# End of layer 0 in a two-layer attention step: gated y chunks loaded two steps ahead, output projection by groups of pairs

## The chip, the cores and the metric

One core of a Trainium2 chip runs the whole program in one launch. The metric is device time in microseconds, lower is better. The kernel before has a median of 2044.95 us over 3 runs (2044.95 to 2046.53).

## The reference, cut to what matters

```
for i in range(2):                       # layer 0: differential attention, layer 1: latent attention
    sh, sc, gt = split(silu(cond) @ w_ada[i] + b_ada[i])     # "ada": 3 x 1024 modulation columns
    h = rmsnorm(x, g_pre[i]) * (1 + sc) + sh
    o = attention_i(h @ w_in)            # 8 heads, 1024 latent and 256 prompt tokens
    y = rmsnorm(o, g_sub) * silu(gate)   # layer 0: per head
    x = x + gt * rmsnorm(y @ w_out[i], g_post[i])
```

Everything is float32. There are 1280 tokens, 1024 columns, 8 heads. Outputs are x after both layers and the keys and values of the prompt.

## The kernel before, in words

Tokens go in five pairs of 128-token tiles: pairs 0 to 3 are latent, pair 4 (`CTXP`) is the prompt. A float32 product is made of three matmuls on a high and a low part (`mm3`, L319 to L321), so each weight tile is loaded into a staging tile `wst` (3 buffers), cast to `wh` on ScalarE (L311), and its rest `wl` is computed on GpSimd or VectorE (L312); `wh` and `wl` have 5 buffers each and one item of work uses 4.

The heads of layer 0 run one after the other. A head has nine units: two for each latent pair and one for the prompt. A unit has scores (L590, L598), row maxima on VectorE (L592, L599), exponentials (L604), the combination of the two softmaxes on VectorE (L635), transposes (L658), their split (L660, L661) and, for each pair, the product with v. In between, a `Feeder` mixes in other matmuls: a list of items, `P2`, each with a planned cost, and every unit gets a share of the planned total in proportion to the weights `FEV`, `FOD`, `FX`. The items are columns of v (`v1`), of the gate (`g0`), modulation chunks (`a0` to `a7`, each 8 matmuls of 32 rows, L185, a copy of their sum on VectorE, L205, and four small matmuls, L230) and last `y3`: the last quarter of the gate, with the y chunks. A modulation matmul is planned at `AC` = 480 ns, three matmuls of a gate column at 360 ns.

A y chunk (`y_chunk`) is 256 columns of a pair: y and the gate are loaded from DRAM (L739), multiplied on GpSimd (L740), transposed on TensorE (L749), and split by ScalarE and VectorE (L750, L751). Fifteen chunks are placed in `y3`, by a table `at` of step counts; five more (the columns of the last two heads) follow, two of them (for pairs 3 and 4) in the output projection, on tiles called `xt`.

The output projection of layer 0 (`out_items`) has four items of 256 columns; each goes over all five pairs, with the weights of the next item requested while the last pair runs. At the last item a pair is complete: x is loaded, the residual is added (`residual`, L952 to L967), x1 is stored (L1514), its norm is taken in place (`norm_pair`, L255 to L262) and a generator of four steps of transposes (`norm_pair_to_hT`, L282 to L291) goes into a queue, `Later`: it may begin `HD` = 28 steps after that, one step in every three, where a step is three matmuls. The first projection of layer 1 (`ev_kva`) then takes the pairs in order and first finishes what the queue still holds for its pair.

The order of instructions on each engine is fixed when the program is built; engines wait for each other by semaphores.

Of the kernel before, what the change touches and what calls it, by code (L numbers as in the profile page):

```python
# [17 lines left out]
P = 128  # L18
D = 1024
# [62 lines left out]
class K:  # L82
    P1 = "k0 q0 k1 q1 k2 q2 k3 q3"
    P2 = "v1 a0 a1 v2 g0 a2 v3 a3 g1 a4 a6 g2 a5 a7 y3"
# [645 lines left out]
    def y_chunk(self, pr, kk, late=None):  # L730
# [12 lines left out]
        if pr not in self.yT:  # L743
# [11 lines left out]
    def gate_y_item(self, hp):  # L755
# [7 lines left out]
        def gen(ws):  # L763
            gs = [self.y_chunk(pr, kk) for pr in range(NPAIR) for kk in range(3)]
            at = [34 + 4 * n for n in range(6)] + [64 + 2 * n for n in range(6)] + [99] * 5

            def step(n):
                if n < len(gs):
                    next(gs[n])
                return next(gs[n - 1]) if 1 <= n < len(gs) + 1 else 0  # L770
            n = cnt = 0
            for v in gate(ws):
                if v is not None:
                    cnt += 1
                    if cnt >= at[n]:
                        v += step(n)
                        n += 1
                yield v
            for n in range(n, len(gs) + 1):
# [3 lines left out]
    def l0_items(self):  # L783
# [5 lines left out]
        def item(x):  # L789
# [5 lines left out]
            if k == "y":  # L795
                return self.gate_y_item(j), 80 * 360 + 15 * 440
# [3 lines left out]
    def l0_heads(self, items):  # L800
# [88 lines left out]
    def gp_rows(self, pool, l, cond, ps, pstag):  # L889

        nc = self.nc
        gp = self.t(pool, [P, D], f"gp{cond if l else 0}")
        for half in range(2):
# [4 lines left out]
            nc.scalar.copy(gp[:, half * 512:(half + 1) * 512], pt.rearrange("p a b -> p (a b)"))  # L898
        return gp
# [759 lines left out]
```

## Time and profile before

| what | value |
|---|---|
| median of 3 runs | 2044.95 us |
| the profiled execution | 2044.24 us, of it a span of 2042.4 us |
| TensorE busy | 1926.0 us (94%) |
| VectorE busy | 1241.2 us (61%) |
| ScalarE busy | 957.9 us (47%) |
| GpSimd busy | 513.1 us (25%) |

TensorE is busy for nearly all of the span, and the chain that ended last runs almost only over it. So the numbers that matter are the gaps on TensorE, and the stretches in which its granted clock is 0.50 of full speed. Times below count from the start of the span. The heads of layer 0 end at about 998 us, the output projection of layer 0 runs to about 1138 us, and the first projection of layer 1 follows it.

### The profile page before, as it was taken

To read this page: it belongs to the slowest core of one execution; us is meant where nothing else is said; L and a number is where in the kernel's file an instruction comes from. 1 tells how busy PE (TensorE), PEld (TensorE's weight loads), DVE (VectorE), ACT (ScalarE), POOL (GpSimd) and SP (SyncE) were. 2 spreads that over 40 slices of the span, in tenths; PEclk is the share of its full clock that TensorE was granted. 3 is DMA by queue.
4 is the path that set the end of the run, shared out by engine and by line. 5 is a ranking of instruction groups with operands and counts; after the bars stand their busy time and mean duration, and the time that the engine had idled before them with its cause. 6 is when DMAs were issued, how large, how long until landed. Compare 5 with 4: busy or idle time off the path is not lost. (4 is left out here: it accounts for less than half of the span.)

```text
span 2042.4 us, 36029 instructions
## 1 busy us (share of the span) xinstructions
PE 1926.0 (94%) x13472; PEld 1732.5 (85%) x13472; DVE 1241.2 (61%) x2503; ACT 957.9 (47%) x2401; POOL 513.1 (25%) x733
## 2 busy tenths in 40 slices
PE   6899999999999999998698899999999999999998
PEld 4788888798988978887698798888999889998998
DVE  4543447788778777788314823247776876777413
ACT  4422124666666666666324633234544444556421
POOL 3354442222122122224313532011000110003214
PEclk8999999999999999999899999999999999999999
DMA  8555544455355353544413212210101001012412
GB/s 305 157 165 187 175 150 145 146 148 146 116 155 184 103 173 113 172 131 140 141 43 115 94 55 68 73 55 21 36 24 32 22 23 41 27 37 91 149 64 104
DMA packets 207086, 220.85 MB, mean 108 GB/s; under 512 B 23776, under 2 KB 171584, under 8 KB 206784
## 3 DMA queue, kind: packets, MB, share of 16 engines
q1 hardware_dynamic: 206608, 218.51, 34.1%
q8 instruction: 106, 1.74, 0.4%
q14 instruction: 68, 0.56, 0.1%
q10 hardware_dynamic: 304, 0.05, 0.0%
HBM read 148.95 MB, written 69.53 MB: 107 GB/s over the span
## 5 line engine op out<-in xcount | busy, mean ns | idle before, releaser
L319 PE MATMUL pj<-wh,hh 128*128 128x256 f32 (+1 forms) x1264 | 368.8, 292 | 5.8 <-DVE hh L290 2.8
L320 PE MATMUL pj<-wl,hh 128*128 128x256 f32 (+1 forms) x1264 | 359.1, 284 | 4.1 <-POOL wl L312 1.8
L321 PE MATMUL pj<-wh,hl 128*128 128x256 f32 (+1 forms) x1264 | 359.7, 285 | 2.0 <-POOL hl L291 1.9
L319 PEld LDWEIGHTS pj<-wh,hh 128*128 128x128 f32 x1264 | 242.1, 192 | 10.9 <-DVE hh L290 4.3
L320 PEld LDWEIGHTS pj<-wl,hh 128*128 128x128 f32 x1264 | 242.5, 192 | 5.5 <-POOL wl L312 3.3
L321 PEld LDWEIGHTS pj<-wh,hl 128*128 128x128 f32 x1264 | 242.0, 191 | 5.0 <-POOL hl L291 3.6
L312 POOL TENSOR_TENSOR wl<-wst,wh 128x512 fp32r<-128x512 f32 (+3 forms) x90 | 104.2, 1166 | 560.2 <-ACT wh L311 456.1
L592 DVE TENSOR_REDUCE mA<-S 128x1 f32<-128x1024 f32 x128 | 155.6, 1219 | 58.4 <-PE S L590 57.7
L321 PE MATMUL pj<-hh,wl 128*128 128x512 f32 (+1 forms) x512 | 188.5, 368 | 0.4 <-POOL wl L352 0.3
L319 PE MATMUL pj<-hh,wh 128*128 128x512 f32 (+1 forms) x512 | 188.3, 368 | 0.0
L320 PE MATMUL pj<-hl,wh 128*128 128x512 f32 (+1 forms) x512 | 187.8, 367 | 0.0
L604 ACT ACTIVATE e<-S,bias 128x1024 f32<-128x1024 f32 x128 | 142.8, 1116 | 93.4 <-DVE bias L601 91.0
L590 PE MATMUL S<-kl,q 128*128 128x512 f32 x512 | 152.9, 419 | 4.6 <-ACT e L604 3.0
L660 ACT CAST pth<-tp 128x512 fp32r<-128x512 f32 (+1 forms) x208 | 99.6, 512 | 84.3 <-PE tp L658 83.4
L660 ACT CAST pth<-pj 128x512 fp32r<-128x512 f32 (+1 forms) x192 | 98.2, 518 | 79.6 <-PE pj L658 78.0
L635 DVE SCALAR_TENSOR_TENSOR e<-e,cf,e 128x512 f32<-128x512 f32 (+1 forms) x192 | 127.1, 700 | 1.1
L661 DVE TENSOR_TENSOR ptl<-tp,pth 128x512 fp32r<-128x512 f32 (+1 forms) x208 | 116.0, 581 | 14.1 <-ACT pth L660 13.4
L243 POOL TENSOR_SCALAR orsv<-oss 128x2 f32<-128x2 f32 x40 | 8.1, 202 | 433.2 <-ACT oT L688 433.1
L661 DVE TENSOR_TENSOR ptl<-pj,pth 128x512 fp32r<-128x512 f32 (+1 forms) x192 | 112.9, 592 | 5.5 <-ACT pth L660 5.2
L658 PE MATMUL pj<-identr,e 128*128 128x128 f32 x640 | 109.1, 279 | 6.9 <-DVE ptl L661 4.0
L321 PEld LDWEIGHTS pj<-hh,wl 128*128 128x128 f32 x512 | 96.3, 188 | 20.3 <-POOL wl L352 3.2
L590 PEld LDWEIGHTS S<-kl,q 128*128 128x128 f32 x512 | 90.8, 196 | 23.4 <-ACT e L604 6.1
(325 smaller groups left out, 5342.1 us busy)
## 6 DMA issues: line engine op xcount, KB each, us to landing
q<-qsd SPq DMA_DIRECT2D x320, 64.0 KB, 2.0
wst<-in_da_w_in_dram SPq DMA_DIRECT2D x64, 256.0 KB, 3.1
kl<-ksd SPq DMA_DIRECT2D x64, 192.0 KB, 3.9
ast<-in_w_ada_dram SPq DMA_DIRECT2D x8, 1024.0 KB, 9.2
wh<-in_w_ada_dram SPq DMA_DIRECT2D x32, 256.0 KB, 2.8
wl<-in_w_ada_dram SPq DMA_DIRECT2D x32, 256.0 KB, 3.1
wst<-in_w_out_dram SPq DMA_DIRECT2D x32, 256.0 KB, 2.6
vdh<-s SPq DMA_DIRECT2D x24, 256.0 KB, 2.1
```

Source lines behind the costliest of these rows:

```text
L243: nc.gpsimd.tensor_scalar(out=v, in0=ss, scalar1=1.0 / n, scalar2=EPS, op0=ALU.mult, op1=ALU.add)
L312: (lo_engs or [nc.gpsimd])[k0 // kb % len(lo_engs or [0])].tensor_tensor(out=wl, in0=st, in1=f32(wh), op=ALU.subtract)
L319: nc.tensor.matmul(out, a[0], b[0], start=first, stop=False)
L320: nc.tensor.matmul(out, a[0], b[1], start=False, stop=False)
L321: nc.tensor.matmul(out, a[1], b[0], start=False, stop=last)
L590: nc.tensor.matmul(S[:, so:so + 512], st(cc, o), kl[cc][:, so:so + 512], start=(o == 0), stop=(o == 1))
L592: nc.vector.reduce_max(out=mA[:, cc:cc + 1], in_=S, axis=AX.X)
L604: nc.scalar.activation(u.es[cc][:, 0:1024], A[cc], AF.Exp, bias=bias[:, cc:cc + 1], scale=0.125, accum_out=u.zA[:, cc:cc + 1])
L635: nc.vector.scalar_tensor_tensor(out=w[:, sl], in0=w[:, sl], scalar=cf, in1=e0[:, sl], op0=ALU.mult, op1=ALU.add)
L658: nc.tensor.transpose(tp[:, j, :], u.e[:, (c0 + j) * P:(c0 + j + 1) * P], self.ident)
L660: nc.scalar.copy(hi, tp[:, 0:cn, :])
L661: nc.vector.tensor_tensor(out=u.ptl[g][:, 0:cn, u.i * P:(u.i + 1) * P], in0=tp[:, 0:cn, :], in1=f32(hi), op=ALU.subtract)
```

## The change

```diff
-    P2 = "v1 a0 a1 v2 g0 a2 v3 a3 g1 a4 a6 g2 a5 a7 y3"
+    P2 = "v1 a0 a1 v2 g0 a2 v3 a3 g1 a4 a5 g2 y3"
+    YA = (6, 7)
+    YS = [32 + 4 * n for n in range(6)] + [60 + 2 * n for n in range(6)] + [78 + 3 * n for n in range(5)]
-    HD, HE = 28, 3
+    HD, HE, ND = 44, 3, 12
-    AC = 480.0
+    AC = 215.0
+    OUT0, OUT1 = ((0, 1, CTXP), (2, 3)), (tuple(range(NPAIR)),)
+    ORD1 = OUT0[0] + OUT0[1]
@@ y_chunk: every second chunk on two of the weights' staging tiles; three steps
+        elif alt:
+            y, g = (self.t(self.wp, [P, 2, 256], "wst", bufs=3) for j in range(2))
         for o, src in ((y, self.ydram), (g, self.gdram)):
             nc.sync.dma_start(...)
+        yield 1
         nc.gpsimd.tensor_tensor(out=y, in0=y, in1=g, op=ALU.mult)
         yield 1
+        if late:
+            yield 1
@@ gate_y_item
-            at = [34 + 4 * n for n in range(6)] + [64 + 2 * n for n in range(6)] + [99] * 5
             def step(n):
-                if n < len(gs):
-                    next(gs[n])
-                return next(gs[n - 1]) if 1 <= n < len(gs) + 1 else 0
+                for j in range(3):
+                    if 0 <= n - j < len(gs):
+                        next(gs[n - j], None)
+                return 440 if n >= 2 else 0
-            for v in gate(ws):
+            for v in self.chain([(lambda: ws, gate)] + more):
@@ l0_heads
-        post, yc, ylist = iter(()), None, list(range(NPAIR))
+        post, yc, ylist = iter(()), None, [0, 1, 2, CTXP, 3]
+            if yc:
+                next(yc)
@@ out_items, l1_tok_item: the pairs of a group, in its order
-                for pr in range(NPAIR):
+                for pr in prs:
-        return [item(n) for n in range(4)]
+        return [item(n, prs) for prs in groups for n in range(4)]
@@ run
+        def load_x(pr):
...
+            x0s[pr] = x0, xt
+        def norm(pr):
             self.norm_pair(xs[pr], yp, sp)
+            yield
+        later, norms, x0s = Later(self.HE), Later(1), {}
+        for prs in self.OUT0:
+            prefetch[2, prs[-1]] = prs[0]
+            prefetch.update({(3, a): b for a, b in zip(prs, prs[1:])})
             if n == 3:
...
                 x_pair(pr, zz, gp)
+                norms.add(norm(pr), self.ND, pr)
+                later.add(turn(pr), self.HD, ("h", pr))
+            if (n, pr) in prefetch:
+                load_x(prefetch[n, pr])
```

The columns of the gate `gp` also become two pieces (768 and 256 wide), and the prompt's are put into tiles of x. The number of matmuls stays the same. Since there are two groups of pairs, the output weights of layer 0 are loaded and split twice: 16 loads of 256 KB more, 16 casts on ScalarE, 8 subtractions on VectorE and 8 on GpSimd.

Three places show how the order moves. In these rows the changed kernel has its own line numbers: L189 is L185 of before, L234 is L230, L594 is L590, L662 is L658, L759 is L749, L908 is L896, L316 is L312, L266 is L262, L978 is L959, L986 is L967.

TensorE, the end of the first modulation chunk, before (`silc` is the conditioning, `sel` adds up the four row groups, `S` are scores):

```order
L185 MATMUL pj_3924<-wh_3652,silc_231 32x512
L658 MATMUL pj_3932<-identr_219,e_3711 128x128 x4
L598 MATMUL pj_3940<-kl_3052,q_3774 128x256 x2
L598 MATMUL pj_3940<-kl_3053,q_3774 128x256 x2
L658 MATMUL pj_3954<-identr_219,e_3711 128x128 x2
L185 MATMUL pj_3924<-wl_3653,silc_231 32x512
L185 MATMUL pj_3924<-wh_3654,silc_231 32x512
L185 MATMUL pj_3924<-wl_3655,silc_231 32x512
L230 MATMUL pj_4004<-sel_234,s_4002 128x2 x4
L185 MATMUL pj_4011<-wh_3983,silc_231 32x512
```

and with the change:

```order
L189 MATMUL pj_3977<-wl_3709,silc_231 32x512
L189 MATMUL pj_3977<-wh_3710,silc_231 32x512
L189 MATMUL pj_3977<-wl_3711,silc_231 32x512
L594 MATMUL S_4030<-kl_3052,q_3765 128x512 x4
L234 MATMUL pj_4004<-sel_234,s_4002 128x2 x4
L189 MATMUL pj_4011<-wh_3983,silc_231 32x512
```

Four score matmuls now stand between the last modulation matmul and the small ones that wait for VectorE's copy of the sum. Over all eight chunks, before, three had nothing in between and the other five 18 to 54 matmuls; with the change one has nothing (the fourth), the others 4, 8, 17, 32, 32, 48 and 60.

TensorE, the end of head 7, before (`kl` are y chunks, `e` the last unit's weights, `pth` and `vh` its product with v):

```order
L896 MATMUL xt_12135<-identr_219,ada_127_236 128x128 x2
L749 MATMUL pj_11960<-identr_219,kl_11923 128x128 x4
L749 MATMUL pj_11967<-identr_219,kl_11850 128x128 x4
L896 MATMUL xt_12135<-identr_219,ada_127_236 128x128
L896 MATMUL xt_12141<-identr_219,ada_127_236 128x128 x4
L749 MATMUL pj_11984<-identr_219,kl_11956 128x128 x4
L658 MATMUL pj_11991<-identr_219,e_11780 128x128 x4
L658 MATMUL pj_11998<-identr_219,e_11780 128x128 x4
L658 MATMUL pj_12005<-identr_219,e_11780 128x128 x2
L749 MATMUL pj_12014<-identr_219,kl_11978 128x128 x4
L749 MATMUL pj_12021<-identr_219,kl_12010 128x128 x4
L319 MATMUL pj_12028<-pth_2521_11854,vh_10961 128x256
```

and with the change:

```order
L189 MATMUL pj_11987<-wl_11924,silc_231 32x512
L189 MATMUL pj_11987<-wh_11925,silc_231 32x512
L189 MATMUL pj_11987<-wl_11926,silc_231 32x512
L189 MATMUL pj_11987<-wh_11927,silc_231 32x512
L759 MATMUL pj_11992<-identr_219,kl_11877 128x128 x4
L189 MATMUL pj_11987<-wl_11928,silc_231 32x512
L662 MATMUL pj_12005<-identr_219,e_11807 128x128 x4
L189 MATMUL pj_11987<-wh_11929,silc_231 32x512
L662 MATMUL pj_12013<-identr_219,e_11807 128x128 x4
L189 MATMUL pj_11987<-wl_11930,silc_231 32x512
L662 MATMUL pj_12020<-identr_219,e_11807 128x128 x2
L323 MATMUL pj_12028<-pth_2523_11881,vh_10963 128x256
```

The two chunks straight ahead of the last product with v are gone from there, and the last modulation chunk (L189) stands between the transposes.

VectorE, where pairs 0 and 1 are complete, before (`xt` and `z` are the two pieces of x, L952 to L967 the residual, L262 the norm; the first two x tiles are pair 0's):

```order
L952 SCALAR_TENSOR_TENSOR rsv_13169<-zss_2592_12180 128x2
L959 SCALAR_TENSOR_TENSOR ztmp_13173<-pj_13110,rs_13171,gp_2569_12134 128x256
L967 SCALAR_TENSOR_TENSOR z_2591_12179<-z_2591_12179,rs_13171,x_2691_13163 128x768
L959 SCALAR_TENSOR_TENSOR ztmp_13177<-pj_13110,rs_13171,gp_2569_12134 128x256
L967 SCALAR_TENSOR_TENSOR z_2591_12179<-z_2591_12179,rs_13171,x_2692_13164 128x768
L262 TENSOR_SCALAR xt_13165<-xt_13165,rs_13195 128x256 x2
L952 SCALAR_TENSOR_TENSOR rsv_13260<-zss_2597_12236 128x2
L959 SCALAR_TENSOR_TENSOR ztmp_13264<-pj_13201,rs_13262,gp_2569_12134 128x256
L967 SCALAR_TENSOR_TENSOR z_2596_12235<-z_2596_12235,rs_13262,x_2708_13254 128x768
L959 SCALAR_TENSOR_TENSOR ztmp_13268<-pj_13201,rs_13262,gp_2569_12134 128x256
L262 TENSOR_SCALAR z_2591_12179<-z_2591_12179,rs_13195 128x768 x2
L967 SCALAR_TENSOR_TENSOR z_2596_12235<-z_2596_12235,rs_13262,x_2709_13255 128x768
```

and with the change:

```order
L986 SCALAR_TENSOR_TENSOR z_2598_12187<-z_2598_12187,rs_12845,x_2673_12784 128x768
L978 SCALAR_TENSOR_TENSOR ztmp_12851<-pj_12790,rs_12845,gp_2576_12141 128x256
L986 SCALAR_TENSOR_TENSOR z_2598_12187<-z_2598_12187,rs_12845,x_2674_12785 128x768
L266 TENSOR_SCALAR xt_12786<-xt_12786,rs_12912 128x256 x2
L971 SCALAR_TENSOR_TENSOR rsv_12934<-zss_2606_12248 128x2
L978 SCALAR_TENSOR_TENSOR ztmp_12938<-pj_12863,rs_12936,gp_2576_12141 128x256
L986 SCALAR_TENSOR_TENSOR z_2605_12247<-z_2605_12247,rs_12936,x_2683_12857 128x768
L978 SCALAR_TENSOR_TENSOR ztmp_12942<-pj_12863,rs_12936,gp_2576_12141 128x256
L266 TENSOR_SCALAR z_2598_12187<-z_2598_12187,rs_12912 128x768 x2
L986 SCALAR_TENSOR_TENSOR z_2605_12247<-z_2605_12247,rs_12936,x_2684_12858 128x768
L316 TENSOR_TENSOR wl_12961<-wst_12962,wh_12960 128x512
L316 TENSOR_TENSOR wl_12973<-wst_12974,wh_12972 128x512
```

Behind the norm of pair 0 and the residual of pair 1 there now come the two low parts of the weights with which the second group begins. On TensorE the first transposes of pair 0 come 132 matmuls after its last projection matmul, where they were 87 behind it.

## Rows read from the trace of the kernel before

**Rows 1.** Busy time by engine in stretches, granted TensorE clock, DMA share.

```profile
core 0: us, PE busy (x) PEld busy (x) DVE busy (x) ACT busy (x) POOL busy (x), PEclk, DMA share, GB/s
410.00:560.00 150.00, 147.64 (x1112) 138.15 (x1112) 123.06 (x251) 100.71 (x268) 30.27 (x60) 1.00 0.47 139
...
850.00:900.00 50.00, 43.52 (x287) 33.63 (x286) 40.72 (x78) 31.28 (x81) 16.32 (x25) 1.00 0.49 153
900.00:968.00 68.00, 60.98 (x458) 55.96 (x456) 54.74 (x101) 43.49 (x109) 23.17 (x34) 1.00 0.47 139
968.00:998.00 30.00, 17.34 (x108) 15.32 (x107) 16.15 (x25) 13.15 (x33) 14.20 (x15) 0.77 0.44 142
...
1015.00:1095.00 80.00, 80.00 (x688) 80.00 (x687) 13.88 (x18) 22.89 (x72) 11.09 (x22) 1.00 0.15 46
1095.00:1176.00 81.00, 65.68 (x502) 62.42 (x502) 59.13 (x126) 49.56 (x129) 43.35 (x58) 0.94 0.37 121
```

**Rows 2.** The same view of the stretches with a granted clock of 0.50.

```profile
389.80:396.60 6.80, 6.80 (x19) 4.44 (x20) 4.72 (x9) 3.52 (x9) 1.27 (x1) 0.50 0.92 297
662.90:669.70 6.80, 6.22 (x22) 5.54 (x23) 4.39 (x8) 4.28 (x10) 0.37 (x1) 0.50 0.82 194
...
778.90:782.30 3.40, 3.40 (x19) 3.40 (x18) 1.80 (x6) 1.56 (x5) 0.01 (x1) 0.50 0.41 115
980.30:994.00 13.70, 8.24 (x39) 7.44 (x38) 4.51 (x7) 3.51 (x6) 6.27 (x5) 0.50 0.66 211
1011.00:1014.40 3.40, 3.02 (x14) 3.02 (x15) 0.75 (x1) 0.69 (x1) 0.61 (x2) 0.51 0.56 175
1110.00:1113.40 3.40, 3.40 (x18) 3.40 (x17) 1.40 (x4) 2.77 (x8) 1.55 (x4) 0.50 0.87 287
1151.00:1157.80 6.80, 6.05 (x29) 6.06 (x30) 4.89 (x14) 5.53 (x18) 4.34 (x9) 0.50 0.36 102
```

**Rows 3.** TensorE's waits, 300 to 850 us: total us, times, longest.

```profile
PE pj L230 <- DVE s L205: 8.6, 3, 3.6
```

**Rows 4.** TensorE in order of time, 850 to 900 us: start, us, idle before.

```profile
867.65 1.20 PE L590 MATMUL S<-kl,q 128*128 128x512 f32 x4 [0.76 <-ACT e L604]
```

**Rows 5.** TensorE's waits, 850 to 968 us.

```profile
PE pj L749 <- POOL kl L740: 3.9, 2, 2.4
```

**Rows 6.** TensorE's waits, 900 to 1015 us.

```profile
PE pj L749 <- POOL kl L740: 11.9, 5, 4.1
PE pj L749 <- POOL xt L740: 4.4, 1, 4.4
...
PE pj L319 <- DVE hl L751: 1.4, 1, 1.4
```

**Rows 7.** GpSimd in order of time, 966 to 1013 us.

```profile
1010.06 1.26 POOL L740 TENSOR_TENSOR xt<-xt,xt 128x512 f32<-128x512 f32 x1 [9.16 <-DMA xt<-g]
```

**Rows 8.** TensorE's waits, 1095 to 1176 us.

```profile
PE xt L282 <- ACT hfull L289: 9.5, 7, 4.5
PE xt L282 <- DVE z L262: 3.9, 2, 3.3
PE pj L320 <- DVE wl L312: 1.6, 1, 1.6
```

**Rows 9.** VectorE in order of time, 1090 to 1180 us.

```profile
1096.29 0.16 DVE L952 SCALAR_TENSOR_TENSOR rsv<-zss 128x2 f32<-128x2 f32 x1 [5.61 <-ACT junk L926]
...
1107.85 1.61 DVE L262 TENSOR_SCALAR z<-z,rs 128x768 f32<-128x768 f32 x2
1109.38 1.01 DVE L967 SCALAR_TENSOR_TENSOR z<-z,rs,x 128x768 f32<-128x768 f32 x1
```

**Rows 10.** Weight splits (L312) of 1015 to 1176 us: ns min/median/max.

```profile
L312 DVE TENSOR_TENSOR wl<-wst,wh x8: 679/912/1754, 1032.1 to 1135.1; 128x512 fp32r<-128x512 f32 x8
```

**Rows 11.** VectorE by shape, softmax combination, 300 to 960 us: count, busy us, mean ns.

```profile
L635 DVE SCALAR_TENSOR_TENSOR e<-e,cf,e 128x512 f32<-128x512 f32 x124 | 94.7, 787 | 1.0
```

**Rows 12.** The same group in 966 to 973 us, beside two GpSimd multiplications (L740).

```profile
L635 DVE SCALAR_TENSOR_TENSOR e<-e,cf,e 128x512 f32<-128x512 f32 x3 | 4.2, 1412 | 0.1
```

More of the change, by code (lines that the diff above doesn't have):

```diff
@@ L728, in pt_tiles, with y_chunk @@
             u.pth, u.ptl = prev.pth, prev.ptl
-    def y_chunk(self, pr, kk, late=None):
+    def y_chunk(self, pr, kk, late=None, alt=False):
         nc, c = self.nc, self.c
@@ L753, in y_chunk, with gate_y_item @@
         yield 440
-    def gate_y_item(self, hp):
+    def gate_y_item(self, hp, more):
         self.gated = -1
@@ L763, in gen @@
         def gen(ws):
-            gs = [self.y_chunk(pr, kk) for pr in range(NPAIR) for kk in range(3)]
-            at = [34 + 4 * n for n in range(6)] + [64 + 2 * n for n in range(6)] + [99] * 5
+            gs = [self.y_chunk(pr, kk, alt=(3 * pr + kk) % 2) for pr in range(NPAIR) for kk in range(3)]
+            at = self.YS
             def step(n):
-                if n < len(gs):
-                    next(gs[n])
-                return next(gs[n - 1]) if 1 <= n < len(gs) + 1 else 0
+                for j in range(3):
+                    if 0 <= n - j < len(gs):
+                        next(gs[n - j], None)
+                return 440 if n >= 2 else 0
             n = cnt = 0
-            for v in gate(ws):
[L773 to L777, printed above, removed]
+            for v in self.chain([(lambda: ws, gate)] + more):
+                cnt += 1
+                while n < len(at) and cnt >= at[n]:
+                    v += step(n)
+                    n += 1
                 yield v
-            for n in range(n, len(gs) + 1):
+            for n in range(n, len(gs) + 2):
                 yield step(n)
@@ L795, in item @@
             if k == "y":
-                return self.gate_y_item(j), 80 * 360 + 15 * 440
+                more = [item(f"a{n}") for n in self.YA]
+                return self.gate_y_item(j, [it for it, _ in more]), 80 * 360 + 15 * 440 + sum(t for _, t in more)
             return self.l0_tok_item(k, j), 80 * 360
@@ L897, in gp_rows, with gp_tile, out_items @@
                                     self.ident)
-            nc.scalar.copy(gp[:, half * 512:(half + 1) * 512], pt.rearrange("p a b -> p (a b)"))
-        return gp
-    def out_items(self, l, yT, zp, pool, sp, pj, gps, after):
+            pv = pt.rearrange("p a b -> p (a b)")
+            for o, a, b in ([(out[0][:, 0:512], 0, 512)] if half == 0 else
+                            [(out[0][:, 512:768], 0, 256), (out[1], 256, 512)]):
+                nc.scalar.copy(o, pv[:, a:b])
+        return out
+    def gp_tile(self, pool, cond):
+        gp = self.t(pool, [P, D], f"gp{cond}")
+        return gp[:, 0:768], gp[:, 768:1024]
+    def out_items(self, l, groups, yT, zp, pool, sp, pj, gps, after):
         nc = self.nc
@@ L976, in gen @@
         def gen(ws):
-            for pr in range(NPAIR):
+            for pr in self.ORD1:
                 before(pr)
@@ L1515, in x_pair, with turn @@
             xs[pr] = [[zz[0][:, i, :], xt[:, i, :]] for i in range(2)]
+        def norm(pr):
             self.norm_pair(xs[pr], yp, sp)
-        later = Later(self.HE)
-        def after(n, pr, tiles, zz):
-            if n == 0 and pr < len(self.ylate):
-                later.add(self.y_chunk(self.ylate[pr], 3, yp), 4, ("y", self.ylate[pr]))
-            if n == 0 and pr < CTXP:
-                later.finish(("y", pr + 1))
+            yield
+        def turn(pr):
+            norms.finish(pr)
+            yield from self.norm_pair_to_hT(xs.pop(pr), 1, pr, big, yp, ps, "xt")
+        later, norms, x0s = Later(self.HE), Later(1), {}
+        prefetch = {}
+        for prs in self.OUT0:
+            prefetch[2, prs[-1]] = prs[0]
+            prefetch.update({(3, a): b for a, b in zip(prs, prs[1:])})
+        def after(n, pr, tiles, zz):
+            i = self.ORD1.index(pr)
+            if n == 0 and i < len(self.ylate):
+                y = self.y_chunk(self.ylate[i], 3, yp)
+                next(y)
+                later.add(y, 4, ("y", self.ylate[i]))
+            if n == 0 and i + 1 < NPAIR:
+                later.finish(("y", self.ORD1[i + 1]))
             if n == 3:
+                gp = gps[0]
                 if pr == CTXP:
-                    later.finish(("h", 1))
-                    gp = self.gp_rows(zp, 0, 1, ps, "xt")
-                x_pair(pr, zz, gp if pr == CTXP else gps[0])
-                later.add(self.norm_pair_to_hT(xs.pop(pr), 1, pr, big, yp, ps, "xt"), self.HD, ("h", pr))
-        gps = {0: self.gp_rows(zp, 0, 0, ps, "xt")}
+                    gp = self.t(yp, [P, 768], "x0", bufs=3), self.t(yp, [P, 2, 256], "xt", bufs=3)[:, 0, :]
+                    self.gp_rows(gp, 0, 1, ps, "xt")
+                x_pair(pr, zz, gp)
+                norms.add(norm(pr), self.ND, pr)
+                later.add(turn(pr), self.HD, ("h", pr))
+            if (n, pr) in prefetch:
+                load_x(prefetch[n, pr])
+        gps = {0: self.gp_rows(self.gp_tile(zp, 0), 0, 0, ps, "xt")}
         self.hT, self.hG = {}, {}
-        its = self.out_items(0, self.yT, zp, yp, sp, c1.pj, gps, after)
+        its = self.out_items(0, self.OUT0, self.yT, zp, yp, sp, c1.pj, gps, after)
         def switch():
@@ L1585, in run @@
                 self.yT_load(pr, 0, H)
-            gps = {j: self.gp_rows(zp, 1, j, ps, "xt") for j in range(2)}
+            gps = {j: self.gp_rows(self.gp_tile(zp, j), 1, j, ps, "xt") for j in range(2)}
             x1 = {}
```

21 lines of the change are left out of this document (11 added, 10 removed).

## The prediction

> **What bounds the kernel now.** I read the busy times by stretch first [rows 1]. From 1015 to 1095 us, the body of the output projection, TensorE works without a gap: 688 matmuls in 80.00 us, 0.116 us each. There nothing can be won without fewer matmuls, and the change has as many as before. In the middle heads it is nearly the same: 147.64 of 150 us from 410 to 560 us, with VectorE at 123.06. The losses sit around the end of layer 0: TensorE stands still for 6.5 us from 850 to 900, 7.0 us from 900 to 968, 12.7 us from 968 to 998, and 15.3 us from 1095 to 1176 (each the length less the busy time). The second view shows what these gaps cost once more [rows 2]: behind a long gap the granted clock is 0.50, which is 1.2 instead of 2.4 GHz, for 3.4 to 13.7 us, and work done there takes twice as long, so half of the busy time inside is lost. The third is TensorE's waits, which say who is late: VectorE's copy behind three modulation chunks [rows 3], GpSimd's multiplication of y chunks [rows 5, 6], and norm and transposes where pairs end [rows 8]. So I add up gaps and lost clock, stage by stage. TensorE's work is only moved and costs nothing by itself.
>
> **Modulation chunks.** Three chunks have no matmul between their sum and the small matmuls, and exactly three waits for that copy stand in the trace, 8.6 us together, 3.6 us the longest [rows 3]. Behind them the clock is low in stretches with 6.80, 6.22 and 3.40 us of work [rows 2], of which 8.2 us are lost. After the change one chunk has no cover (3.6 us stays), one has four score matmuls, which take 1.2 us [rows 4] and leave 2.4 us, one has eight and leaves 1.2 us; the others have 17 and more. Together 7.2 us stay, so 1.4 us go; of the lost clock I keep one long and one short stretch, 3.4 and 1.7 us, so 3.1 us go. Sum: 4.5 us. Bounds: nothing at all, since VectorE's queue may be longer at the new places, and 13.2 us (16.8 less the one uncovered wait).
>
> **The stretch 850 to 900 us** holds the last two modulation chunks, with TensorE at 43.52 of 50 us. Two chunks move to the end of head 7 and matmuls of the gate take their place; those keep TensorE 98% busy elsewhere. I take half of the 6.5 us, 3.2 us, between 0 and 6.5.
>
> **y chunks in head 7.** Loading a step earlier and multiplying a step before the transposes gives each chunk one more step of cover. Two waits of 3.9 us stand before 968 us [rows 5]; 0.9 us stays, 3.0 us go. Three more, 11.9 less 3.9 = 8.0 us, stand from 968 to 998 us, with 1.4 us for the first projection matmul, which waits for the split of the last chunk [rows 6]. In the new order the last chunks before the projection belong to the prompt pair, which is third in it. The low clock there holds 8.24 us of work, so 4.1 us are lost [rows 2]. Together 13.5 us; as the last modulation chunk now waits for VectorE in this same place, I leave 2.5 us, so 11.0 us go. If the chunks come no earlier than now, nothing goes.
>
> **The late chunk.** The 4.4 us wait [rows 6] is for pair 3, whose y is written last; its multiplication starts at 1010.06 after 9.16 us of waiting for its load [rows 7]. Now the prompt pair's chunk is first. Its y is long written, but its load stands behind the last y store in SP's queue, so only part of the wait goes: of 4.4 us and 1.5 us of clock (half of 3.02, [rows 2]) I take 3.5 us, between 0 and 5.9.
>
> **Ends of pairs.** Before, pair 0's transposes follow its last matmul by 87 matmuls, 10.1 us. Its norm is ready 13.2 us after the first residual instruction (1096.29 to 1109.46, [rows 9]) and that starts about 1 us after the last matmul: 14.2 us, 4.1 us too late, which is the 3.9 us wait [rows 8]. With 132 matmuls, 15.3 us, it is just in time. The 9.5 us for ScalarE's copies [rows 8] come from five pairs' steps on top of residuals; three of the pairs now have the whole second group to spread over. I keep 3.0 us of them, because four steps of one pair still follow each other as closely. With 1.6 us for a weight split this is 15.0 us, and 4.7 us of lost clock (half of 3.40 and 6.05, [rows 2]): 19.7 us. There is a new wait: on VectorE the low parts of the second group's first weights stand behind pair 0's norm and pair 1's residual. By the row of before that is 14.1 us after pair 0's first residual instruction (1110.39), 15.1 after its last matmul, and a split takes 0.9 us [rows 9, 10], so 16.0 us; TensorE gets there after 96 matmuls and some 7 more, 12.0 us. The wait is 4.0 us, and 1.7 us for a low clock. So 19.7 - 3.0 - 5.7 = 11.0 us go. Bounds: 0, and 17.7 if the split comes in time and steps cost 2.0.
>
> **The second loading of the output weights.** From 1015 to 1095 us ScalarE works 22.89 and VectorE 13.88 of 80 us, and DMA has a share of 0.15 [rows 1], so 16 casts, 16 subtractions and 16 loads are hidden. If that cover is gone, the price is a wait such as the 1.6 us [rows 8] at each of four more boundaries, 6.4 us. I take 0. The load of x a pair ahead frees a wait that the trace does not show on TensorE: 0. The two-piece gate rows cost three more short ScalarE copies for each use: 0, hidden in the same way.
>
> **GpSimd beside VectorE.** A softmax combination of 512 columns takes 787 ns in the heads [rows 11] but 1412 ns where two y multiplications run beside it [rows 12]. Before, the last multiplications come after the last combination; now they come earlier, beside some. Each unit has two such halves, so 1.25 us more per unit, 10.0 us if all eight units of head 7 are hit. VectorE has 13.3 us free from 900 to 968 [rows 1], so I charge 4.0 us, between 0 and 10.0. The Trainium skill, "GPSIMD Engine Reference", section "Specifications", says that GpSimd's SBUF interfaces are shared with VectorE and contend with VectorE instructions that have two SBUF inputs; these rows agree. By that rule alone all eight units would be hit and the sum would be 6.0 us smaller.
>
> **The sum** is 4.5 + 3.2 + 3.0 + 11.0 + 3.5 + 11.0 - 4.0 = 32.2 us. The profiled execution took 2044.24 us, 0.7 below the median of the runs shown, so 2012.0 us. Its own range, with terms off by a few us each, is 2003 to 2022.
>
> **Rivals.** First, contention and the last units' own chain take the place of the chunk waits: VectorE is what head 7 ends on. Then 6.0 us more of slow combinations, and half of the 14.0 us at the chunks stays: 2025. For it speaks the doubling of the row; against it, that VectorE idles for 13.9 of 30 us in the stretch 968 to 998. The skill's rule above would lead here. Chance 0.15.
>
> Second, the pace. Planning a modulation matmul at 215 instead of 480 ns makes the planned work behind head 0's first units 214.8 instead of 231.7 us, so the fill per head falls from 29.0 to 26.9 us. If VectorE sets the pace of the middle heads, six of them do not shrink, and 2.1 us each, 12.7 us, come back as gaps: 2025. Against it: 2.4 us of gaps in 150 us, VectorE at 82%. Chance 0.12.
>
> Third, all goes better: no contention, no split wait, chunks fully covered, 44 us of the 66 in the stages: 2000. Chance 0.10.
>
> Fourth, slower: weight splits become the bound. The order puts VectorE's half of each weight item behind whatever residual or norm came first, an item of the second group lasts only 11.1 us (96 matmuls), and there are seven boundaries between items. If at each TensorE waits as long as the longest now, 4.5 us [rows 8], and loses 3.0 us of clock (half of 6.05), that is 52.5 us, less the 5.7 counted: 2059. It decides from a loss of 6.2 us at each of the six other boundaries (37 us above the forecast). Against it: no gap at any boundary from 1015 to 1095 us. Chance 0.07.
>
> Fifth, a half of that together with the first rival leaves no change, 2041 to 2049. Chance 0.06. That the change does not do what it says is excluded by the order, which shows every step of it moved.
>
> **How the numbers follow.** The forecast keeps 0.50. A measurement of this kernel can tell 0.2%, 4.1 us, from no change. Faster by more: 0.50 + 0.15 + 0.12 + 0.10 = 0.87; within: 0.06; slower: 0.07. The range takes in the first two rivals with a margin above, and the third below: 1999 to 2034; the last two, 0.13, and some tails stay out.
>
> **What would show it.** TensorE's waits on L740 and L749 are below 3 us in all; the stretch from the last product with v of pair 2 to the first projection matmul shrinks from 30 to about 18 us. Behind modulation chunks one long wait stays, the fourth. One wait of about 4 us for a weight split stands where the second group begins, and the transposes wait for ScalarE in all for about 3 us. The prediction is wrong if gaps between 300 and 850 us grow beyond 25 us, or if several boundaries of the projection show waits for splits.

## The result, and the profile after

The change takes 2019.99 us in the median of 4 runs (2016.65 to 2026.26); before takes 2044.95 (2044.29 to 2046.53, 4 runs). The ratio is 0.9875, 95% interval 0.9856 to 0.9894: 25.0 us faster, where 32.2 were forecast, and 8 us above the predicted 2012.0, inside the range. The profiled execution of the change is its slowest run: 2026.26 us, a span of 2024.3. Its stages, cut at the same matmuls in both traces (first score matmul of head 0 and of head 7, first projection matmul, then 960, 240 and 240 projection matmuls):

| stage, us | before | change | difference | forecast |
|---|---|---|---|---|
| up to head 0 | 321.8 | 324.3 | +2.5 | 0 |
| heads 0 to 6 | 557.8 | 552.6 | -5.2 | -4.5 |
| head 7, to the first projection matmul | 118.8 | 99.6 | -19.2 | -13.2 |
| output projection, layer 0 | 133.0 | 144.2 | +11.2 | with the next two: -14.5 |
| first projection of layer 1 | 48.7 | 39.6 | -9.1 | |
| the next 240 matmuls | 29.7 | 31.3 | +1.6 | |
| the rest | 832.6 | 832.6 | 0.0 | 0 |

So the heads gave more than forecast and the projections (the three rows from the output projection on) gave nothing: 211.5 us became 215.1. (The table counts the 3.2 us forecast for 850 to 900 us with head 7. Of the gaps in that stretch before, 6.48 us, 4.25 lie ahead of head 7, which begins at 879 us.) The traces are single executions. Where kernels below have the same code in a stage, heads 0 to 6 take 551.8 to 556.1 us (nine traces), head 7 97.5 to 100.1 us (six) and the projections 208.5 to 215.1 us (five). The profiled execution of the change is the longest of the five there, so a difference of less than about 4 us in the heads, or 7 us in the projections, says little.

Busy times by stretch show the same, in the order of [rows 1]. The columns are the stretch, its length, and each engine's busy time with its count; the last three are granted clock, DMA share and GB/s:

```profile
core 0: us, PE busy (x) PEld busy (x) DVE busy (x) ACT busy (x) POOL busy (x), PEclk, DMA share, GB/s
408.00:558.00 150.00, 147.47 (x1112) 137.76 (x1111) 125.55 (x250) 100.40 (x266) 33.18 (x64) 1.00 0.47 134
...
877.00:968.00 91.00, 85.42 (x614) 73.86 (x613) 79.44 (x153) 63.93 (x164) 33.27 (x50) 0.98 0.58 176
968.00:977.00 9.00, 8.99 (x65) 7.24 (x64) 4.77 (x9) 4.34 (x10) 5.32 (x5) 1.00 0.39 131
977.00:1055.00 78.00, 71.81 (x593) 71.40 (x591) 17.39 (x27) 25.78 (x77) 21.25 (x31) 0.96 0.37 117
1055.00:1095.00 40.00, 29.36 (x209) 28.09 (x210) 33.29 (x58) 23.50 (x64) 19.45 (x22) 0.87 0.49 158
```

The end of head 7, where TensorE was busy for 17.34 of 30 us, now has 8.99 of 9. The gaps have moved to 1055 to 1095 us, where the first group's pairs end: 29.36 of 40, at a mean clock of 0.87. The stretches at half clock answer to [rows 2]:

```profile
760.50:763.90 3.40, 3.40 (x11) 1.60 (x10) 0.00 (x0) 0.26 (x1) 0.00 (x0) 0.51 1.02 366
948.30:951.70 3.40, 3.40 (x13) 2.82 (x12) 2.87 (x4) 1.89 (x5) 0.00 (x0) 0.50 0.96 304
989.20:996.00 6.80, 5.49 (x26) 5.49 (x27) 0.81 (x2) 1.64 (x5) 2.54 (x2) 0.50 0.58 197
1057.50:1064.30 6.80, 4.87 (x23) 4.88 (x24) 3.92 (x7) 3.54 (x11) 2.23 (x5) 0.50 0.77 247
1088.20:1091.60 3.40, 3.40 (x18) 3.40 (x18) 2.88 (x8) 2.68 (x8) 0.73 (x1) 0.50 0.23 77
1139.40:1142.80 3.40, 2.85 (x14) 2.86 (x15) 1.87 (x6) 2.19 (x7) 2.02 (x4) 0.50 0.01 2
```

Four of the six lie behind 977 us, where the output projection begins. TensorE's waits (total us, times, longest), first for 300 to 850 us, against [rows 3], then for 975 to 1180 us, against [rows 6, 8]:

```profile
PE pj L189 <- DMA wh<-in_w_ada_dram: 3.8, 3, 2.3
...
PE pj L234 <- DVE s L209: 0.9, 1, 0.9
...
PE xt L286 <- ACT hfull L293: 10.0, 5, 3.4
PE pj L759 <- POOL xt L748: 4.2, 1, 4.2
PE pj L324 <- DVE wl L316: 3.7, 2, 3.3
PE pj L323 <- ACT wh L315: 2.7, 1, 2.7
PE tp L1018 <- DVE kva L1031: 1.5, 2, 1.0
```

The wait behind modulation chunks fell from 8.6 to 0.9 us; new are 3.8 us for the chunks' weights from DRAM (0.3 before). From 850 to 977 us no matmul waits for a product of GpSimd any more, where before there were 11.9 us [rows 6]. Behind that, the waits did not shrink: 9.5 us for ScalarE became 10.0, 4.4 us for the late chunk became 4.2, and the 3.9 us for the norm made way for 6.0 us at the second group's first weights (1055.75 and 1059.43 us).

**The late chunk.** SP's queue and GpSimd, 978 to 992 us:

```profile
980.77 0.37 SPq L699 DMA_DIRECT2D y<-y  x1
981.19 1.78 SPq L1040 DMA_DIRECT2D gk<-in_mla_g_kva_dram  x1
983.06 0.39 SPq L745 DMA_DIRECT2D xt<-y  x1
983.50 0.46 SPq L745 DMA_DIRECT2D xt<-g  x1
...
989.20 1.26 POOL L748 TENSOR_TENSOR xt<-xt,xt 128x512 f32<-128x512 f32 x1 [8.45 <-DMA xt<-g]
```

The load is issued at 983, behind the last y store and a load that nobody is in a hurry for, and GpSimd waits 8.45 us, where it waited 9.16 [rows 7]. In this execution nothing is won by loading another pair's chunk. The wait differs from trace to trace: in the nine that have this late chunk in the projection it is 0 to 5.0 us, 2.7 in the mean, and 4.4 and 5.0 in the two with the projection of before.

**Where the second group starts.** VectorE, then ScalarE, 1044 to 1061 us:

```profile
1051.26 0.62 DVE L266 TENSOR_SCALAR xt<-xt,rs 128x256 f32<-128x256 f32 x2 [4.95 <-DMA x<-xt]
1051.79 0.15 DVE L971 SCALAR_TENSOR_TENSOR rsv<-zss 128x2 f32<-128x2 f32 x1
...
1056.72 2.05 DVE L986 SCALAR_TENSOR_TENSOR z<-z,rs,x 128x768 f32<-128x768 f32 x1
1058.69 1.28 DVE L316 TENSOR_TENSOR wl<-wst,wh 128x512 fp32r<-128x512 f32 x2
...
1054.25 0.84 ACT L259 ACTIVATE junk<-z 128x768 bf16<-128x768 f32 x1 [5.30 <-DVE z L986]
1055.00 0.18 ACT L259 ACTIVATION_READ_ACCUMULATOR junk<-z 128x1 f32 x1
1055.10 0.60 ACT L315 CAST wh<-wst 128x512 fp32r<-128x512 f32 x1
```

Pair 0's norm works in place, so it waits until the store of x1 has read its tile: 4.95 us in which VectorE stands still, with pair 1's residual (L971) behind it. ScalarE waits 5.30 us for that residual, with the next group's cast (L315) behind it. VectorE's low parts (L316) come last. Both halves of the first weights are late by one chain. (An experiment below queues the norm later: ScalarE's half is then in time, VectorE's is not.)

**The transposes.** ScalarE, GpSimd and VectorE, 1080 to 1089 us, around the wait at 1087.53 (2.8 us):

```profile
1086.45 1.02 ACT L293 ACTIVATE hfull<-xt,ada 128x256 f32<-128x256 f32 x2 [2.79 <-POOL hl L295]
...
1085.69 0.73 POOL L295 TENSOR_TENSOR hl<-hfull,hh 128x256 fp32r<-128x256 f32 x1 [1.03 <-DVE hh L294]
...
1082.09 1.15 DVE L266 TENSOR_SCALAR z<-z,rs 128x768 f32<-128x768 f32 x2 [0.87 <-POOL rs L249]
1083.15 1.67 DVE L266 TENSOR_SCALAR xt<-xt,rs 128x256 f32<-128x256 f32 x2
1084.74 0.68 DVE L951 TENSOR_TENSOR z<-pj,gp 128x512 f32<-128x512 f32 x1
1085.34 0.48 DVE L294 CAST hh<-hfull 128x256 fp32r<-128x256 f32 x2
```

TensorE's wait is put down to ScalarE, but ScalarE waits for a tile that GpSimd has yet to read, GpSimd for VectorE's high part (L294), and that stands in VectorE's queue behind the norm of a later pair (L266). The late one is VectorE, by its order. The longest of the five waits, 3.38 us at 1139.95, has the same chain: there the high part stands behind an instruction of the next projection (L1031) that waited 3.91 us for GpSimd. Together these are 6.2 of the 10.0 us.

### The profile page after: what moved, and what is told of

Read it like the earlier page. It is cut to its first block, busy times and chain, and to the rows that moved or that the text cites. A ratio compares the mean times of both kernels' runs of the same rounds, so it can differ in the third digit from the quotient of the medians.

```text
span 2024.3 us, 36143 instructions
## 1 busy us (share of the span) xinstructions
PE 1925.5 (95%) x13472; PEld 1729.8 (85%) x13472; DVE 1255.1 (62%) x2511; ACT 965.1 (48%) x2421; POOL 520.4 (26%) x741
## 5 line engine op out<-in xcount | busy, mean ns | idle before, releaser
L316 POOL TENSOR_TENSOR wl<-wst,wh 128x512 fp32r<-128x512 f32 (+3 forms) x98 | 113.0, 1161 | 582.2 <-ACT wh L315 485.8
L594 PE MATMUL S<-kl,q 128*128 128x512 f32 x512 | 149.3, 411 | 6.0 <-ACT e L608 5.6
L665 DVE TENSOR_TENSOR ptl<-tp,pth 128x512 fp32r<-128x512 f32 (+1 forms) x208 | 116.2, 582 | 14.1 <-ACT pth L664 13.3
L665 DVE TENSOR_TENSOR ptl<-pj,pth 128x512 fp32r<-128x512 f32 (+1 forms) x192 | 113.3, 594 | 12.6 <-ACT pth L664 12.1
L315 ACT CAST wh<-wst 128x512 fp32r<-128x512 f32 (+3 forms) x140 | 78.5, 573 | 79.1 <-issue 21.8
L324 PEld LDWEIGHTS pj<-hl,wh 128*128 128x128 f32 x512 | 96.3, 188 | 16.9
L662 PE MATMUL pj<-identr,e 128*128 128x128 f32 x640 | 106.5, 277 | 4.2 <-DVE s L496 1.2
```

Source lines behind the costliest of these rows:

```text
L315: nc.scalar.copy(wh, st)
L316: (lo_engs or [nc.gpsimd])[k0 // kb % len(lo_engs or [0])].tensor_tensor(out=wl, in0=st, in1=f32(wh), op=ALU.subtract)
L324: nc.tensor.matmul(out, a[0], b[1], start=False, stop=False)
L594: nc.tensor.matmul(S[:, so:so + 512], st(cc, o), kl[cc][:, so:so + 512], start=(o == 0), stop=(o == 1))
L662: nc.tensor.transpose(tp[:, j, :], u.e[:, (c0 + j) * P:(c0 + j + 1) * P], self.ident)
L665: nc.vector.tensor_tensor(out=u.ptl[g][:, 0:cn, u.i * P:(u.i + 1) * P], in0=tp[:, 0:cn, :], in1=f32(hi), op=ALU.subtract)
```

## The experiments

All kernels were timed beside the kernel before on the same chip; its medians there were 2046.43, 2045.48, 2045.20 and 2045.51 us. The 95% intervals reach 2 to 8 us to each side, so a difference of less than about 5 us between two of these kernels is not certain. The ratios are to the kernel before; the change has 0.9875 (0.9856 to 0.9894).

**Which half of the change.** The first kernel has the heads' half alone, the second the projection's half alone.

```diff
  before, with P2, YA, YS, AC, y_chunk, gate_y_item and l0_heads of the change
```

> The kernel before with the first half of the change alone: the new place of the last two modulation chunks, their planned cost of 215 ns, y chunks in three steps on two kinds of buffers; the output projection stays as before. Theory A (nearly all of the gain comes from the heads; the profiles put -5 us on heads 0 to 6 and -18.5 us on head 7, and +3.6 us on the projection): 2021 us, between 2018 and 2025. Rival B (the profiled run of the change was its slowest, and the projection by groups pays about 10 us in the others): 2030 us or more.

Measured: 2020.92 us (2019.22 to 2023.92), ratio 0.9874 (0.9847 to 0.9902). The whole gain is here.

```diff
  the change, with P2, AC, y_chunk's two steps, gate_y_item and l0_heads of before
```

> The change with its first half undone: heads as before, output projection by two groups of pairs with x ahead and norm and transposes later. Theory A: within 5 us of before, 2040 to 2050 us. Rival B: 2034 us or less.

Measured: 2045.24 us (2042.70 to 2049.00), ratio 0.9997 (0.9985 to 1.0008). The projection's half is worth nothing that can be seen, alone or with the other. In its trace the projections take 208.5 us, against 211.5, and head 7 takes 120.9 us against 118.8.

**Parts of the heads' half.**

```diff
-                for j in range(3):
+                for j in range(2):
                     if 0 <= n - j < len(gs):
                         next(gs[n - j], None)
-                return 440 if n >= 2 else 0
+                return 440 if n >= 1 else 0
```

with load and multiplication in one step.

> The changed kernel (2020.0 us), but each y chunk of the heads is loaded and multiplied in one step and transposed in the next, as before the change; the places in the order, the staging tiles and the sequence of the pairs stay. Theory A (the third step is what took the waits for GpSimd's products away): at least half of the 11.9 + 3.9 us of waits for them come back in head 7, 8 to 14 us with the clock lost behind them: 2027 to 2034. Rival B (it is the new places, with the prompt's chunks last and the modulation chunks between them, that give the cover): less than 3 us come back: 2019 to 2023.

Measured: 2026.88 us (2026.23 to 2029.81), ratio 0.9914 (0.9897 to 0.9930): 6.9 us slower than the change, at the near edge of A, though not as A has it. (The expectation adds 3.9 to 11.9 us; the 11.9 contain the 3.9.) Head 7 takes 104.4 us instead of 99.6, but no chunk of the heads waits for GpSimd: the time is in short waits for VectorE and ScalarE, 1.5 us the longest; both traces have 3.4 us at half clock there. So the third step is worth something, but the long waits stay away without it. Whether the new places or the new tiles keep them away, this run does not separate.

```diff
-    P2 = "v1 a0 a1 v2 g0 a2 v3 a3 g1 a4 a5 g2 y3"
-    YA = (6, 7)
+    P2 = "v1 a0 a1 v2 g0 a2 v3 a3 g1 a4 a6 g2 a5 a7 y3"
+    YA = ()
```

> The changed kernel (2020.0 us), but the last two modulation chunks are back ahead of the last quarter of the gate, at the order of before; three-step y chunks stay. Theory A (these two chunks at the end of head 7 are the cover for the last chunks and units, and their place of before cost gaps from 850 to 900 us): 3.2 us come back there and 4 to 8 us of waits at the last units: 2027 to 2031. Rival B (only the loads a step earlier count, the place of the modulation does nothing): 2018 to 2022.

Measured: 2032.58 us (2030.91 to 2033.03), ratio 0.9937 (0.9921 to 0.9953): 12.6 us slower, 1.6 beyond A's range and far from B. Its trace has 7.8 us more in head 7 (107.4 us) and 3.0 more in heads 0 to 6. TensorE's waits, 879 to 980 us, show what the two chunks had covered:

```profile
PE pj L759 <- POOL kl L748: 2.6, 1, 2.6
PE pj L662 <- DVE hl L761: 2.4, 3, 1.6
PE pj L759 <- DVE ptl L665: 1.7, 2, 1.5
PE pj L759 <- DVE hl L761: 1.4, 1, 1.4
```

Without them the last chunks and the last unit's transposes wait for each other's splits. The edit also leaves the last steps of the table `YS` nothing to count, so the last chunks follow each other at once; the run takes away both the cover and the spacing. Of the three parts set back singly this costs most.

```diff
-    AC = 215.0
+    AC = 480.0
```

> The changed kernel (2020.0 us), with a modulation matmul planned at 480 ns again instead of 215 ns. Theory A (the new price puts more matmuls between a chunk's sum and the small matmuls and spreads the other work evenly; this is what took 5.0 us off the heads before the last): 2 to 6 us slower, in the stretch of heads 0 to 6: 2022 to 2026. Rival B (the order of the items does that by itself, the price nothing): 2018 to 2021.5.

Measured: 2027.13 us (2023.01 to 2032.86), ratio 0.9914 (0.9890 to 0.9938), 7.1 us slower, 1 us beyond A, with an interval that just meets the change's. TensorE's waits, 300 to 850 us:

```profile
PE pj L234 <- DVE s L209: 8.2, 3, 3.6
```

That is the row of before (8.6, 3, 3.6) [rows 3], with the new order of items. So the price sets the cover of a modulation chunk, not the order. The kernel with the modulation chunks back at their old places shows the converse: with the new price and the old order the wait is 0.9 us. Half clock follows: between 330 us and head 7 the three traces with the old price have three or four such stretches, the eleven with the new one have one or two. Where A puts the time is not shown: heads 0 to 6 take 555.4 us here, inside the range of the kernels with the new price.

**The projection.**

```diff
-    OUT0 = ((0, 1, CTXP), (2, 3))
+    OUT0 = ((0, 1, CTXP, 2, 3),)
-    ORD1 = OUT0[0] + OUT0[1]
+    ORD1 = OUT0[0]
```

> The change with a single group of pairs, in the order 0, 1, prompt, 2, 3: the output weights of layer 0 are loaded once, everything else stays. Theory A (the wait at the start of the second group is new, 6.0 us and half of 6.8 us of low clock): that wait goes, the ends of five pairs crowd together again and wait about as long as before the change; 2018 to 2026 us. Rival B (the groups are what pays in the projection): 2030 us.

Measured: 2027.23 us (2025.24 to 2028.78), ratio 0.9907 (0.9884 to 0.9931), 7 us slower than the change, between the expectation's two cases, with an interval that just meets the change's. In its trace the projections take 218.7 us against 215.1, with one wait for ScalarE of 6.9 us. But the kernel with the heads' half alone, which also loads the weights once and keeps the projection of before, is 6.3 us faster than this one. So the two groups, if they are worth these 7 us, only make up for what the rest of the projection's half (the order of the pairs, norms and transposes later) loses in one group.

```diff
-    HD, HE, ND = 44, 3, 12
+    HD, HE, ND = 44, 3, 24
```

> The change with the norm of a pair queued 24 steps after its end instead of 12. Theory A (at the start of the second group VectorE stands behind the norm of pair 0, which waits 4.95 us for the store of x, and pair 1's residual and the weight splits stand behind it): the waits of 2.7 and 3.3 us at the start of the second group fall below 2 us in all and the low clock with them, 6 to 9 us less than the change, 2011 to 2014 us. Rival C (the first weights are late because their buffers come free only with the last matmuls of the group before): no difference, 2020 us.

Measured: 2015.32 us (2014.27 to 2018.56), ratio 0.9852 (0.9828 to 0.9877). This is 4.7 us faster than the change, between A and C, and the intervals meet. At the second group's start 2.8 us of the 6.0 stay. A new wait of 5.3 us stands at 1066.42 us, in the midst of pair 0's transposes. VectorE there:

```profile
1061.65 1.61 DVE L266 TENSOR_SCALAR z<-z,rs 128x768 f32<-128x768 f32 x1 [4.73 <-POOL rs L249]
...
1064.23 0.48 DVE L294 CAST hh<-hfull 128x256 fp32r<-128x256 f32 x2
```

Pair 1's norm waits 4.73 us for GpSimd, which adds the prompt pair's residual (4.33 us, L984) ahead of it, and the high part that pair 0's transposes need stands behind that norm.

```diff
-        post, yc, ylist = iter(()), None, [0, 1, 2, CTXP, 3]
+        post, yc, ylist = iter(()), None, [0, 1, CTXP, 2, 3]
...
-                later.add(y, 4, ("y", self.ylate[i]))
+                later.add(y, 30, ("y", self.ylate[i]))
```

> The changed kernel (2020.0 us), but the prompt pair's last chunk is done in the heads and the last chunks of pairs 2 and 3, which the projection needs only in its second group, in the projection, 30 steps later than asked now. Theory A (the wait of 4.2 us early in the projection is for that chunk's load, which stands behind the last y store): it goes, and 3.4 us of clock (half of the 6.8 us at half clock) with it: 2011 to 2015. Rival B (the three chunks now placed in the heads make the wait there, with the last y that they need): 2018 to 2023.

Measured: 2021.80 us (2017.00 to 2023.67), ratio 0.9881 (0.9858 to 0.9905): no gain in the median, in B's range for the time. In its trace the 4.2 us wait and its half clock are gone, as A has it, and the output projection takes 137.4 us instead of 144.2, but the two behind it take 3.4 us more, where new stretches at half clock stand. That the wait is for this load is shown, what it is worth is not.

```diff
-                full = self.t(pool, [P, 256], "hfull", bufs=3 - l)
+                full = self.t(pool, [P, 256], "hfull", bufs=4 - l)
```

> The changed kernel (2020.0 us) with three instead of two tiles for the normalised, transposed columns that ScalarE writes and from which VectorE and GpSimd make the two parts. Theory A (the four waits of the transposes for ScalarE, 9.7 us, are waits for one of these two tiles, which GpSimd's low part holds behind its residual additions and weight splits): a third tile takes at least half of the 9.7 us and one of the stretches at half clock: 2011 to 2016. Rival B (the four steps of a pair follow too closely for ScalarE itself, as the prediction had it): the waits stay: 2018 to 2023.

Measured: 2019.50 us (2013.68 to 2024.30), ratio 0.9874 (0.9833 to 0.9915). TensorE's waits, 975 to 1180 us:

```profile
PE xt L286 <- ACT hfull L293: 8.6, 6, 2.6
```

8.6 us against 10.0: theory A falls. Six traces with this projection and two tiles have 7.6 to 11.3 us here, so no effect of the third tile can be seen. That fits a wait in which VectorE's high part, not GpSimd's low part, is the late one.

```diff
-    HD, HE, ND = 44, 3, 12
+    HD, HE, ND = 44, 5, 12
```

> The changed kernel (2020.0 us) with one step of transposes in every five steps instead of every three. Theory A of the third tile (GpSimd's queue holds the tile at random places, spacing only helps in part): 2 to 5 of the 9.7 us go: 2015 to 2019. Rival B (spacing is all): the waits go down to 2 us and the half clock behind them with them: 2009 to 2014. Rival C (pairs 2 and 3 now end so late that the first projection of layer 1 must finish their steps at once): no gain or a loss, 2020 to 2026.

Measured: 2018.46 us (2015.66 to 2020.04), ratio 0.9867 (0.9838 to 0.9896). The same row reads:

```profile
PE xt L286 <- ACT hfull L293: 6.6, 5, 2.4
```

With spacing the wait is a little below those six traces, and the 240 matmuls behind the first projection of layer 1 take 36.4 us instead of 31.3. The median is in A's range, 1.5 us below the change, which is not certain. Neither tiles nor spacing are the cause by themselves.

**Repairs together.** The last two kernels put the prompt's last chunk into the heads, take the third tile, and move norms and transposes of the first group apart:

```diff
-    HD, HE, ND = 44, 3, 12
+    HD, HE, ND = (60, 44), 3, 24
```

> Four repairs together on the changed kernel: the prompt's last chunk in the heads (4.5 us in the trace), the norms 24 steps after a pair (4.7 us), the transposes of the first group's pairs 60 steps after it, so that the norm is done, and the third tile. If the terms add up, 4.5 + 4.7 + 5 = 14 us: 2006, between 2003 and 2010. Rival (what is taken from one wait shows up in the next, as it did in the projection before): 2012 to 2018.

Measured: 2010.92 us (2009.25 to 2014.60), ratio 0.9834 (0.9804 to 0.9864), just above the range for terms that add up and below the rival's; its interval still meets the change's.

```diff
-    HD, HE, ND = (60, 44), 3, 24
+    HD, HE, ND = (72, 44), 3, (36, 24)
```

> The four repairs of the run before (2010.9 us), with the norms of the first group's pairs 36 instead of 24 steps after them and their transposes 72 instead of 60. On VectorE the two low parts of the second group's first weights now stand ahead of pair 0's norm, behind pair 1's residual alone. Theory A (the 2.8 us that TensorE still waits there, and half of the 6.8 us at half clock behind it, come from that norm): they go, 2003 to 2008. Rival (pair 1's residual alone makes the low part as late, or the norms now press on the transposes): 2009 to 2014.

Measured: 2008.38 us (2004.96 to 2011.52, 5 runs), ratio 0.9815 (0.9802 to 0.9829): faster than the kernel before and, with intervals apart, than the change; it lies between A and the rival. Against the run before it the gain of 2.5 us is not certain; the two intervals overlap. Its waits, 975 to 1180 us:

```profile
PE pj L324 <- DVE wl L316: 6.1, 3, 3.1
PE xt L286 <- ACT hfull L293: 2.2, 2, 1.1
```

ScalarE's 10.0 us are down to 2.2. The third tile alone left 8.6 us, spacing 6.6, later norms 9.5, and the four repairs of the run before 6.2. So it takes norms and transposes moved together; no run does that without the third tile and the moved chunk. The wait at the second group's first weights is gone but for 0.4 us, and two others stand at the next two boundaries (2.6 and 3.1 us, at 1061.03 and 1080.79). The projections take 198.8 us, 12.7 below before; head 7, which holds a chunk more, takes 102.7 us, 3.1 more than in the change.

## Why the prediction was right in sign and range, and where it was off

**Modulation chunks (4.5 us).** Heads 0 to 6 gave 5.2 us, but that the two numbers are so close is in part luck. The chunk without cover waits 0.9 us, not 3.6, and those with four and eight score matmuls do not wait: the sum took VectorE's copy to come as late as in the longest wait of before, and it came earlier. The 3.8 us of waits for the chunks' own weights (0.3 before) it did not see. Together 4.2 us of waits went, where 1.4 were forecast. Between 330 us and head 7, before had four stretches at half clock with 19.8 us of work, the three of [rows 2] and this one:

```profile
758.40:761.80 3.40, 3.40 (x10) 1.30 (x10) 2.54 (x6) 0.00 (x0) 1.68 (x3) 0.51 0.52 189
```

The change has one with 3.40 (760.50, above), so 8.2 us of lost clock went, where 3.1 were forecast. That makes 12.4 us, and the stage shrank by 5.2 alone. Part of the difference is TensorE's own work. From its start to the next start, gaps left out and at full clock, a modulation matmul takes 0.26 us in the mean of those that the trace lists, before 0.22: some 3 us for the 96 listed in these heads. It is 0.25 to 0.27 us in the eleven kernels with the new price and 0.21 to 0.22 in the three with the old; why, no run shows. The price as the cause of the waits is shown by the run that sets it back. What it is worth in time is not.

**Head 7 (3.2 + 3.0 + 11.0 - 4.0 = 13.2 us).** It gave 19.2 us. Two sizes were off. The move of two modulation chunks got 3.2 us as an entry for 850 to 900 us; putting them back costs 12.6 us, 7.8 of them in head 7 by the trace, since they are the cover for the last units, which the prediction counted under y chunks. And the contention term of -4.0 us did not come. The combination of 512 columns in head 7, first before (879 to 995 us), then with the change (877 to 974 us), and the one of these 18 that met a multiplication:

```profile
L635 DVE SCALAR_TENSOR_TENSOR e<-e,cf,e 128x512 f32<-128x512 f32 x18 | 16.2, 918 | 0.2
...
L639 DVE SCALAR_TENSOR_TENSOR e<-e,cf,e 128x512 f32<-128x512 f32 x18 | 14.1, 803 | 0.2
...
928.79 1.76 DVE L639 SCALAR_TENSOR_TENSOR e<-e,cf,e 128x512 f32<-128x512 f32 x1
```

So these 18 got 2.1 us shorter. The 1412 ns of [rows 12] are a mean of two that ran beside GpSimd's work (1.73 and 1.75 us) and one that did not (0.75 us). A combination that meets a multiplication thus costs about 1.0 us more, but few do: three of 18 before, one of 18 with the change, though 15 multiplications lie in its head 7. The result that the prediction gave for the Trainium skill's rule ("GPSIMD Engine Reference", section "Specifications"), all eight units hit, is not what this trace shows; that the two engines get in each other's way when they meet, which the page does state, agrees with the row at 928.79.

**The late chunk (3.5 us).** This step failed by its size. The prediction saw that the load stands behind the last y store, and then took most of the wait as gone. In the profiled execution the wait went from 4.4 to 4.2 us and the half clock behind it from 3.02 to 5.49 us of work, 1.2 us more lost: a loss of 1.0 us. In the mean of the nine traces with this late chunk the wait is 2.7 us, so a part of it does go, as the prediction said, but a smaller one.

**Ends of pairs (11.0 us).** This is the step that failed most. It kept 3.0 of the 9.5 us for ScalarE, because three pairs would have the whole second group to spread over; 10.0 us stand there, and 7.6 to 11.3 us in the six traces with this projection. The work did spread, but norms of later pairs were spread into it, on the engine that is late. The new wait at the second group's weights was right in place and kind, and 6.0 us instead of 4.0. The row of before from which its 14.1 us were read has a wait of VectorE for the x1 store inside it:

```profile
1103.93 0.61 DVE L262 TENSOR_SCALAR xt<-xt,rs 128x256 f32<-128x256 f32 x2 [3.20 <-DMA x<-xt]
```

Those 3.20 us became 4.95, and pair 1's last residual instruction takes 2.05 us (1056.72, above) where it took 1.01: 2.8 us more in the chain. With 1.5 us at L1018 (0.4 before) these waits are 17.9 us against 15.4, and the clock loses 5.6 us (half of 4.87, 3.40 and 2.85) against 4.7: 3.4 us lost where 11.0 were to go.

**The second loading of the weights (0).** As casts, subtractions and loads it is hidden, and two groups with it beat one group by 7 us. But the 6.0 us at the second group's start are a wait for weights that one group would not load again; the sum has this price under ends of pairs.

**The rivals.** The first (contention, head 7 ending on VectorE) and the second (middle heads held to VectorE's pace) did not come: head 7 has no such chain, and heads 0 to 6 shrank. The third, with everything better, did not come either, since the projections gave nothing. The fourth, with splits late at every boundary, came at one of seven, apart from 0.4 us. The fifth leaves no change and falls with the time. Of the prediction's own signs, the stretch from the last product with v of pair 2 to the first projection matmul went from 30.2 to 17.6 us, as said, the one long wait behind a modulation chunk is at the fourth, though 0.9 us long, and one boundary waits. The waits for y chunks are 4.2 us, not below 3, all of it the late chunk. The transposes' 10.0 us instead of 3 is the sign that failed.

The profiled execution has 18.1 us less span than before, 7 less than the medians differ, of which 2.5 us lie ahead of head 0. That run and the one of before are single executions, so the terms above are good to a few us. By these traces the heads gave 6.7 us more than their terms and the projections 18.1 us less, so the time lies inside the range in part because errors of both signs met.

## What to carry to other kernels

Put work without dependencies between the last links of a chain: two small modulation chunks there, taken away, cost 12.6 us, the finer staging of the chunk loads 6.9. Before counting a wait as spread out, follow it past the engine that the trace names: here ScalarE was named, and the late one was VectorE, two queues further, behind work for another pair. When a load stands behind a store in one queue, changing which tile it loads gains little; the wait went when the chunk was not needed there any more.

## What the runs showed of the hardware that was not expected

In this trace a VectorE instruction with one input from SBUF is held too while GpSimd adds; the prediction had this for two inputs alone. Two casts, 0.48 us elsewhere (1085.34 above), and GpSimd beside them, 1062 to 1072 us of the change:

```profile
1069.06 2.13 DVE L294 CAST hh<-hfull 128x256 fp32r<-128x256 f32 x2
...
1069.22 1.82 POOL L984 TENSOR_TENSOR z<-z,x 128x768 f32<-128x768 f32 x1 [0.90 <-DVE z L982]
```

The first cast takes 0.28 us. The second begins 0.04 us behind the addition, takes 1.93 us and ends at 1071.19, just behind the addition's end at 1071.04. The Trainium skill, "SBUF — State Buffer", section "Terms", says that the two engines share a port pair that one holds for a whole instruction while the other is blocked; the row agrees, and the cost here is 1.65 us for the pair. The prediction charged contention to the y chunks alone; here the prompt pair's residual additions paid it.
